# Decoder step on one core: last roundings of W_a on VectorE, first remainders of W_o on GpSimd, x in pairs, and a new order of norm and gate work

## The chip, the core and the metric

The kernel runs on one core of a Trainium2 chip. Five engines work side by side: PE (TensorE, matrix products), DVE (VectorE), ACT (ScalarE), POOL (GpSimd) and SP (SyncE, which here issues most of the loads and stores). Each takes its own instructions in the order written into the program, and waits where one needs something that another engine or a transfer has not delivered. The metric is device time in microseconds (us) of one launch; lower is better.

## The reference

One layer of a decoder for a prompt of 1024 tokens and 8 single-token samples, width 1024, all in 32-bit floats:

```
h  = RMSNorm(x) * (1 + scale1) + shift1
z  = h @ w_in                      # q,k,v, gates ga and gb, ...
y_a = W_a( gated delta rule )      # w_gdn_out
y_b = W_b( sliding-window attention )
x  = x + gate1 * W_o( sigmoid(ga) * y_a + sigmoid(gb) * y_b )
h2 = RMSNorm(x) * (1 + scale2) + shift2
x  = x + gate2 * W_down( silu(causal_dwconv3(h2 @ W_gate)) * (h2 @ W_up) )
final RMSNorm, and the new states
```

## The kernel before

Activations lie transposed: 128 partitions are 128 of the 1024 channels, a tile index j or k counts the 8 groups of channels, and the free axis holds the 1032 tokens (1024 of the prompt, 8 samples). W_a works in three parts of 384, 384 and 264 tokens (`PARTS`, t = 0, 1, 2), W_o in four quarters of 256, 256, 260 and 260 (`QUARTERS`, q). Two quarters are a half: `x1[0]` and `x1[1]` hold the residual of the two halves, 8 tiles each.

Every product is made in split form: an operand is taken apart into a rounding (hi, written as fp32r) and a remainder (lo = x − hi), and a product is three matmuls, hi·hi, hi·lo and lo·hi (`mm3`). The helper `split` issues the two steps: the rounding on ACT (L129), the remainder on DVE or on an engine that is passed to it (L130). In the profile a line of such a helper stands for many places, so the tile names tell the place: `wh`, `wl` are weights, `w` and `pk` weights or rooms of W_o and of the feed-forward part, `bmh` and `bml` the roundings and remainders of W_o's input, `mm` an accumulator in PSUM.

The stretch that the change touches has four pieces, one after the other:

1. The end of W_a (`ya_out` in `branches`). After each product of tile j and part t, DVE multiplies it by the gate (`sgx`), adds y_b's share into `t`, and `split` writes the rounding and remainder of the sum into `self.mix[q]`, one piece for each quarter that the part covers. That is `bmh` and `bml`: part 2 covers the last 4 columns of quarter 2 and all of quarter 3.
2. W_o (`output_pass`), quarter by quarter, 8 tiles in each. In quarter 0 each tile's weight is loaded too (`output_weights`, 512 KB into one of three `raw` buffers) and split: tile 0 into `w0` and `w1` in two halves of 512 columns, tile 2 into `w2` and `w3`, the others into rooms of `pk` that later hold other things. x's tile comes in by a load of its own (128 KB, L1431), is added to, and goes out to `x1d` (L1441). Tile 0's product in quarter 0 takes its three kinds of matmul in another order (L1439), the hi weights first.
3. The second norm (`second_norm`), for each quarter as a stream beside W_o: matmuls with ones sum the squares, DVE makes the mean (`rs`), POOL raises it to −1/2 (`power`, L125), DVE spreads it over a diagonal (`dg`, L1505), PE turns that into a row for all partitions (`nr`, L1506), and DVE and ACT scale x. `ffn_states` loads the convolution state (L1565) and transposes it on PE (`wv`, 128x88).
4. The gate and up projections (`ffn_gate_up`), which use seven products of sums and differences for a pair of weight tiles and a half of the tokens (`pair_product`). The seven operands of a half come from `operands`, those of the weights from `pair_weights`, whose sums (`ws`, L1589) are made on POOL for the gate weights.

These streams are written one after the other and given priorities (`weave`); a scheduler then merges them into one order for each engine, by its own cost estimates. So an instruction's place on an engine is not where it stands in the code. `issue_after` ties one instruction behind another on the scheduler's side.

Of the kernel before, what the change touches and what calls it, by code (L numbers as in the profile page):

```python
# [9 lines left out]
F32 = mybir.dt.float32  # L10
# [3 lines left out]
ALU = mybir.AluOpType  # L14
# [50 lines left out]
class Step:  # L65
# [56 lines left out]

    def power(self, out, in_, expo):
        e = expo[:in_.shape[0], :]
        self.nc.gpsimd.tensor_tensor(out, in_, e.broadcast_to(list(in_.shape)), op=ALU.pow)  # L125

    def split(self, hi, lo, x, eng=None):

        self.nc.scalar.activation(hi, x, AF.Copy)  # L129
        (eng or self.nc.vector).tensor_tensor(lo, x, hi.bitcast(F32), op=ALU.subtract)  # L130

    def load_split(self, pool, shape, src, tags, bufs, raws, home=None, raw=None):

# [1198 lines left out]
    def branches(self, pool, pool2):  # L1332
        nc, I = self.nc, self.I
        first = self.part_rooms(pool2, 0)
        ob = {**self.obX, 1: self.load_part(pool2, self.ob, 1)}
        ub = [self.t(pool, [P, KC, n], f"t{t}", bufs=1) for t, (_, n) in enumerate(PARTS)]
        samples, rows = self.sample_delta(pool2), self.last_rows()
        gate = lambda src, j, t: self.gate_part(pool if src is self.sga and j > 5 else self.gt[0], src[j][:, PARTS[t][0]:PARTS[t][0] + PARTS[t][1]], t)

        def yb_out(t, ps):  # L1340
            nc.vector.tensor_tensor(ub[t][:, j, :], ps, gate(self.sgb, j, t), op=ALU.mult)

        def ya_out(t, ps):
            u, v = ub[t][:, j, :], gate(self.sga, j, t)
            nc.vector.tensor_tensor(v, ps, v, op=ALU.mult)
            nc.vector.tensor_tensor(u, u, v, op=ALU.add)
            r0, n = PARTS[t]
            for q, (lo, m) in enumerate(QUARTERS):
                c, e = max(lo, r0), min(lo + m, r0 + n)
                if c < e:  # L1350
                    self.split(*(x[:, j, c - lo:e - lo] for x in self.mix[q]), u[:, c - r0:e - r0])
# [24 lines left out]
        self.bctx.close()  # L1376
        self.bm = self.pool("bm", 1, side="right")
        self.mix = [tuple(self.t(self.bm, [P, KC, QW], f"bm{x}{q}", F32R)[:, :, :n] for x in "hl")
                    for q, (_, n) in enumerate(QUARTERS)]
        for j0 in (0, 2, 4, 6):  # L1380
            w = [self.load_w(I["w_gdn_out"][0][:, j * P:(j + 1) * P]) for j in (j0, j0 + 1)]
            if 0 < j0 < 6:
                for j in (j0, j0 + 1):
                    self.project(w[j - j0], oa, ya_out)
                continue

            for ts in ((0,), (2,), (1,)) if j0 == 0 else ((0,), (1,), (2,)):
                for j in (j0, j0 + 1):
                    self.project(w[j - j0], oa, ya_out, ts)
# [17 lines left out]
    def output_pass(self, pool, q):  # L1407

        nc = self.nc
        lo, n = QUARTERS[q]  # L1410
        x1 = self.x1[q // 2][:, :, lo - HALF[q // 2][0]:][:, :, :n]

        def add(t, ps):
            self.add_gated(t, ps, j, 16)
            sq = self.t(pool, [P, QW], "nsq" if j else "nss", bufs=2)[:, :n]
            if q == 3 and j > 4:
                nc.vector.tensor_tensor(sq, x1[:, j, :], x1[:, j, :], op=ALU.mult)
            else:
                nc.scalar.activation(sq, x1[:, j, :], AF.Square)
            if j == 0:  # L1420
                self.squares[q] = [sq]
            elif j < 6:
                s = self.squares[q][0]
                nc.vector.tensor_tensor(s, s, sq, op=ALU.add)
            else:
                self.squares[q].append(sq)

        for j in range(8):
            if q == 0:
                self.wo.append(self.output_weights(j))  # L1430
            nc.sync.dma_start(x1[:, j, :], self.xT[j][:, lo:lo + n])  # L1431
            if q or j:
                self.project(self.wo[j], self.mix, add, parts=(q,), cols=QUARTERS)
            else:
                ps = self.t(self.next_mm(), [P, 512], "mm")[:, :n]
                (wh, wl), (xh, xl) = self.wo[0], self.mix[0]
                for i in range(3 * KC):
                    w, x, k = (wh, (xh, xl)[i % 2], i // 2) if i < 2 * KC else (wl, xh, i - 2 * KC)
                    nc.tensor.matmul(ps, w[:, k, :], x[:, k, :], start=i == 0, stop=i == 3 * KC - 1)  # L1439
                add(0, ps)  # L1440
            nc.sync.dma_start(self.x1d[j][:, lo:lo + n], x1[:, j, :])  # L1441
            yield

    def output_weights(self, j):

        src = self.I["w_o"][0][:, j * P:(j + 1) * P]
        raw = self.t(self.pw, [P, NP], "raw", bufs=3)
        self.nc.sync.dma_start(raw.rearrange("p (k c) -> p k c", k=KC), src.rearrange("(k p) c -> p k c", p=P))
        if j in (0, 2):
            w = [self.t(self.pw, [P, NP], tag, F32R, bufs=1) for tag in (f"w{j}", f"w{j + 1}")]  # L1450
        else:
            room = self.room(("pk0", "", "pk1", "pk2", "pk3", "pk4", "pk5")[j - 1], [P, KC * QW])
            w = room[:, :NP], room[:, NP:2 * NP]
        for c in (0, 512) if j == 0 else (slice(None),):
            c = c if j else slice(c, c + 512)
            self.split(*(x[:, c] for x in w), raw[:, c])
        return [x.rearrange("p (k c) -> p k c", k=KC) for x in w]

    def x1_cols(self, j, c, n):
# [19 lines left out]
    def second_norm(self, pool, psum, t):  # L1479
# [19 lines left out]
        for w, c0, c1 in ((P, 0, 2), (n - 2 * P, 2, nc_)):  # L1499
            if c0 < c1:  # L1500
                nc.vector.tensor_scalar(rs[:w, c0:c1], ss[:w, c0:c1], 1.0 / NP, EPS, op0=ALU.mult, op1=ALU.add)
        self.power(rs[:, :nc_], rs[:, :nc_], self.mhalf)
        yield
        dg = self.t(pool, [P, 3, P], "dg", bufs=1)[:, :nc_]
        nc.vector.tensor_tensor(dg, bc(self.ident, 1, nc_), bc(rs[:, :nc_], 2, P), op=ALU.mult)  # L1505
# [15 lines left out]
    def operands(self, pool, p, stage):  # L1521
# [18 lines left out]
        self.split(*ops[3], a1)  # L1540
        yield
        minus(d, b2, a1)
        self.split(*ops[2], d)
        yield
        minus(b1, b2, b1)
        self.split(*ops[4], b1)
        yield
        minus(a2, a2, d)
        self.split(*ops[5], a2)
        yield  # L1550
        self.split(*ops[6], b2)
        yield


# [19 lines left out]
        yield  # L1574
        nc.vector.tensor_tensor(sp, sp, bc(fcw[:, 3, :], 1, NS), op=ALU.add)

    def pair_weights(self, pool, w, f, eng=None):


        raw = []  # L1580
# [14 lines left out]
            self.split(t[:, 0], t[:, 1], x)  # L1595
            return t[:, 0], t[:, 1]

        out = [put(a0), put(b0)]
        s1 = calc(a1, b1, ALU.add)
        s2 = calc(s1, a0, ALU.subtract)  # L1600
        out += [put(s2), put(s1)]
        s3 = calc(a0, a1, ALU.subtract)
# [50 lines left out]
    def ffn_gate_up(self, pool, pool2, psum, f, w, first):  # L1653
# [9 lines left out]
        def gate(p, i, q, ps, r):  # L1663
            lo, n = QUARTERS[2 * p + q]
            zq = z[i][:, 2 + lo:2 + lo + n]
            if r is None:
                nc.scalar.copy(zq, ps)
            else:
                nc.vector.tensor_tensor(zq, ps, r, op=ALU.add)
            done[p, i] = done.get((p, i), 0) + 1  # L1670
            if done[p, i] == 2:
                conv(p, i)
# [19 lines left out]
            ss, r = self.norm_at  # L1692
            self.pair_product(psum, w, (0,), gate, {2: ss, 4: r})
        self.pair_product(psum, w, (1,) if first else (0, 1), gate)
        w = self.pair_weights(pool, I["w_ffn_up"][0], f, nc.vector if first else None)

        def up(p, i, q, ps, r):
            lo, n = QUARTERS[2 * p + q]
# [210 lines left out]
    def second_half(self):  # L1909

        nc, S = self.nc, ExitStack
        with S() as c:
# [6 lines left out]
            with S() as right:  # L1919
                xr = self.pool("xr", 1, ctx=right, side="right")  # L1920
                with S() as left:
                    xl = self.pool("xl", 1, ctx=left)
                    self.x1 = [self.t(pl, [P, KC, n], "x1") for pl, (_, n) in zip((xl, xr), HALF)]
                    self.x1d = self.t(self.dr, [KC, P, NT], "x1d")
                    self.squares, self.X, self.wo = {}, {}, []
# [151 lines left out]
```

## Time and profile before

| | us |
|---|---|
| median of 3 runs | 2076.88 (2074.53 to 2081.3) |
| the profiled execution | 2076.01 |
| its span | 2074.3 |
| PE busy | 2008.0 (97%) |
| PE waits for `dg` at L1506 | 3.0, once |
| PE waits for ACT's `w` at L1439 | 2.1, once |

The span runs from the first to the last instruction; 1.7 us of the execution lie around it. A row of the timeline has start, duration, engine, line, operation, out<-in and shape; a bracket behind it gives how long the engine was idle before it and what released it.

### The profile page before, as it was taken

What the parts mean: (1) busy time and instruction counts of PE and PEld (TensorE: products, weight loads), DVE (VectorE), ACT (ScalarE), POOL (GpSimd) and SP (SyncE); (2) the same over time, 40 slices, a digit from 0 to 9 for tenths busy, and PEclk for the clock granted to TensorE, in tenths of its full rate; (3) what the DMA queues carried; (4) which work ended last, traced back from release to release, by engine and by line L of the source; (5) the groups of instructions that cost most, each with busy time, mean ns of one, the idle gap of its engine ahead of it and who ended that gap; (6) DMA issues with size and microseconds to landing.
All of it is one profiled execution on the core that took longest, in us unless ns stands there. A gap on an engine that the chain in (4) does not pass through costs nothing.

```text
span 2074.3 us, 41298 instructions
## 1 busy us (share of the span) xinstructions
PE 2008.0 (97%) x16245; PEld 1905.2 (92%) x16245; DVE 1356.4 (65%) x2714; ACT 902.5 (44%) x2233; POOL 522.1 (25%) x594
## 2 busy tenths in 40 slices
PE   7999999999999999989989999999999999999998
PEld 4987877799999999979989999999999999999997
DVE  4755767483655746656554575479886777668866
ACT  4664545443334343442442452345544444444443
POOL 2000000131321211211111000004556556543561
PEclk9999999999999999999999999999999999999999
DMA  8256443332322322312276774513333332388783
GB/s 293 72 145 207 138 168 116 96 99 65 82 82 57 77 69 52 91 37 61 67 198 184 253 231 133 146 58 90 105 98 103 107 95 91 126 280 280 265 285 115
DMA packets 301887, 275.75 MB, mean 133 GB/s; under 512 B 59730, under 2 KB 248111, under 8 KB 301676
## 3 DMA queue, kind: packets, MB, share of 16 engines
q1 hardware_dynamic: 295642, 252.14, 39.7%
q0 software_dynamic: 5552, 20.37, 2.8%
q8 instruction: 127, 2.08, 0.4%
q14 instruction: 68, 0.56, 0.1%
q10 hardware_dynamic: 498, 0.61, 0.1%
HBM read 212.93 MB, written 62.51 MB: 133 GB/s over the span
## 4 chain that ended last, share of the span: by engine, by line
PE 82%; DMA 6%; DVE 6%; ACT 3%; issue 1%; SPq 1%; POOL 0%; DVEq 0%; POOLq 0%; ACTq 0%
PE mm L180 18%; PE mm L181 18%; PE mm L182 18%; PE wv L180 3%; PE wv L182 3%; PE wv L181 3%; PE wy L182 2%; PE wy L180 2%; PE wy L181 2%; PE pv L652 1%; DMA raw<-in_w_swa_out_dram 1%; PE pt L190 1%; PE tp L190 1%; PE mm L264 1%; PE sc L614 1%
## 5 line engine op out<-in xcount | busy, mean ns | idle before, releaser
L180 PE MATMUL mm<-b1h,wh 128*128 128x384 f32 (+1 forms) x1520 | 496.9, 328 | 4.0 <-ACT gt L1294 1.6
L181 PE MATMUL mm<-b1l,wh 128*128 128x384 f32 (+1 forms) x1520 | 489.1, 323 | 0.0
L182 PE MATMUL mm<-b1h,wl 128*128 128x384 f32 (+1 forms) x1520 | 487.7, 323 | 0.4 <-DVE wl L130 0.3
L180 PEld LDWEIGHTS mm<-b1h,wh 128*128 128x128 f32 x1520 | 286.5, 189 | 13.1 <-issue 4.6
L181 PEld LDWEIGHTS mm<-b1l,wh 128*128 128x128 f32 x1520 | 286.8, 189 | 4.4 <-issue 4.0
L182 PEld LDWEIGHTS mm<-b1h,wl 128*128 128x128 f32 x1520 | 286.0, 188 | 4.5 <-issue 2.8
L129 ACT ACTIVATE wh<-raw 128x1024 fp32r<-128x1024 f32 x83 | 87.1, 1050 | 124.4 <-PE mm L181 72.0
L130 DVE TENSOR_TENSOR wl<-raw,wh 128x1024 fp32r<-128x1024 f32 x82 | 101.9, 1244 | 59.8 <-ACT wh L129 58.9
L181 PE MATMUL mm<-pk,w 128*128 128x260 f32 (+1 forms) x440 | 124.3, 283 | 1.1 <-DVE pk L130 1.1
L180 PE MATMUL mm<-pk,w 128*128 128x260 f32 (+1 forms) x440 | 124.3, 283 | 0.0
L182 PE MATMUL mm<-pk,w 128*128 128x260 f32 (+1 forms) x440 | 124.1, 282 | 0.0
L130 DVE TENSOR_TENSOR w<-ws,w 128x512 fp32r<-128x512 f32 x88 | 78.2, 890 | 36.0 <-ACT w L129 35.8
L1626 ACT COPY bml<-mm 128x256 f32<-128x256 f32 (+1 forms) x132 | 48.9, 371 | 97.6 <-PE mm L182 94.5
L180 PE MATMUL mm<-bmh,w 128*128 128x260 f32 (+1 forms) x320 | 90.3, 282 | 0.0
L182 PE MATMUL mm<-bmh,w 128*128 128x260 f32 (+1 forms) x320 | 90.1, 282 | 0.0
L1681 DVE SCALAR_TENSOR_TENSOR fa<-fz,fcw,fa 128x512 f32<-128x512 f32 x88 | 74.5, 867 | 18.1 <-ACT fa L1679 17.8
L180 PE MATMUL mm<-b2h,wh 128*128 128x384 f32 (+1 forms) x256 | 83.2, 328 | 3.0 <-ACT wh L129 2.9
L181 PEld LDWEIGHTS mm<-pk,w 128*128 128x128 f32 x440 | 82.8, 188 | 1.3 <-DVE pk L130 1.3
L181 PE MATMUL mm<-b2l,wh 128*128 128x384 f32 (+1 forms) x256 | 83.6, 327 | 0.4 <-DVE b2l L130 0.4
L180 PEld LDWEIGHTS mm<-pk,w 128*128 128x128 f32 x440 | 82.9, 188 | 0.2 <-ACT bml L1626 0.2
L182 PEld LDWEIGHTS mm<-pk,w 128*128 128x128 f32 x440 | 82.9, 189 | 0.0
L182 PE MATMUL mm<-b2h,wl 128*128 128x384 f32 (+1 forms) x256 | 82.9, 326 | 0.0
(645 smaller groups left out, 5889.9 us busy)
## 6 DMA issues: line engine op xcount, KB each, us to landing
raw<-in_w_in_dram SPq DMA_DIRECT2D x59, 512.0 KB
ws<-in_w_ffn_down_dram SPq DMA_DIRECT2D x55, 256.0 KB
raw<-xd SPq DMA_DIRECT2D x47, 258.0 KB
raw<-in_w_ffn_down_dram SPq DMA_DIRECT2D x47, 256.0 KB
raw<-in_w_ffn_gate_dram SPq DMA_DIRECT2D x22, 512.0 KB
raw<-in_w_ffn_up_dram SPq DMA_DIRECT2D x22, 512.0 KB
qst<-in_w_mod_dram SPq DMA_DIRECT2D x16, 512.0 KB
raw<-in_w_mod_dram SPq DMA_DIRECT2D x16, 512.0 KB
```

The lines of the kernel that those rows point to most:

```text
L129: self.nc.scalar.activation(hi, x, AF.Copy)
L130: (eng or self.nc.vector).tensor_tensor(lo, x, hi.bitcast(F32), op=ALU.subtract)
L180: mm(ps, whi, xhi, start=first, stop=False, **kw)
L181: mm(ps, whi, xlo, start=False, stop=False, **kw)
L182: self.last_mm = mm(ps, wlo, xhi, start=False, stop=last, **kw).ins
L190: self.nc.tensor.transpose(out, in_, self.ident[:p, :p])
L264: nc.tensor.matmul(ps[32 * j:32 * j + 32], self.cT[:, k0 + j, :], ws[j // 2][:, j % 2, :], start=k0 == 0, stop=k0 > 0)
L614: self.scored = nc.tensor.matmul(sc[:, r, 256 - w:256], q, KH[:, lo:lo + w], start=True, stop=False)
L652: nc.tensor.matmul(pv[64 * r:64 * r + 64], V[:, n - back, ch], ps[:, r::2, :], start=back == 0, stop=back == (n > 0))
L1626: self.last_copy = nc.scalar.copy(r[p, i], x[p])
L1681: nc.vector.scalar_tensor_tensor(ai[:, c:e], zi[:, j + c:j + e], col(j), ai[:, c:e], op0=ALU.mult, op1=ALU.add)
```

## The change

Five edits go together.

- In W_a's last part (t = 2) the tiles j = 6 and 7 no longer round on ACT: DVE writes the rounding itself, as a second sum with an fp32r output, and then the remainder. Other tiles are as before.
- The remainders of W_o's tiles 0 and 1 go to POOL instead of DVE.
- x is loaded two tiles at a time (256 KB and 260 KB), at even j.
- In the gate weights' first use, a weight sum is tied behind the second quarter's `power`.
- The seven gate operands of the second half are tied together in the order in which the products take them: the third operand first, the fifth and sixth behind it, the seventh last. Two copies out of PSUM in the first gate product move from ACT to DVE, one addition waits for the last square of the norm, and one operand of the first up weight waits for the third operand.

```diff
     def split(self, hi, lo, x, eng=None):
-        self.nc.scalar.activation(hi, x, AF.Copy)
-        (eng or self.nc.vector).tensor_tensor(lo, x, hi.bitcast(F32), op=ALU.subtract)
+        return (self.nc.scalar.activation(hi, x, AF.Copy),
+                (eng or self.nc.vector).tensor_tensor(lo, x, hi.bitcast(F32), op=ALU.subtract))
+    def behind(self, made):
+        stack = ExitStack()
+        for x in made:
+            stack.enter_context(self.tc.issue_after(x.ins))
+        return stack
...
         def ya_out(t, ps):
             u, v = ub[t][:, j, :], gate(self.sga, j, t)
             nc.vector.tensor_tensor(v, ps, v, op=ALU.mult)
...
+            if t < 2 or j < 6:
+                nc.vector.tensor_tensor(u, u, v, op=ALU.add)
+                for rooms, a, b, m in spans:
+                    self.split(*(x[:, j, a:a + m] for x in rooms), u[:, b:b + m])
+                return
+            for (hi, _), a, b, m in spans:
+                nc.vector.tensor_tensor(hi[:, j, a:a + m], u[:, b:b + m], v[:, b:b + m], op=ALU.add)
             nc.vector.tensor_tensor(u, u, v, op=ALU.add)
+            for (hi, lo), a, b, m in spans:
+                nc.vector.tensor_tensor(lo[:, j, a:a + m], u[:, b:b + m], hi[:, j, a:a + m].bitcast(F32), op=ALU.subtract)
...
-            nc.sync.dma_start(x1[:, j, :], self.xT[j][:, lo:lo + n])
+            if j % 2 == 0:
+                nc.sync.dma_start(x1[:, j:j + 2, :], self.xT[j:j + 2, :, lo:lo + n].rearrange("k p n -> p k n"))
...
-            self.split(*(x[:, c] for x in w), raw[:, c])
+            self.split(*(x[:, c] for x in w), raw[:, c], None if j > 1 else self.nc.gpsimd)
...
-        self.power(rs[:, :nc_], rs[:, :nc_], self.mhalf)
+        self.factors.append(self.power(rs[:, :nc_], rs[:, :nc_], self.mhalf))
...
-        self.split(*ops[2], d)
+        made = self.split(*ops[2], d)
         yield
-        minus(b1, b2, b1)
-        self.split(*ops[4], b1)
+        self.third = made if p else ()
+        with self.behind(self.third):
+            minus(b1, b2, b1)
+            self.split(*ops[4], b1)
         yield
-        minus(a2, a2, d)
-        self.split(*ops[5], a2)
+        with self.behind(self.third):
+            minus(a2, a2, d)
+            made = self.split(*ops[5], a2)
         yield
-        self.split(*ops[6], b2)
+        with self.behind(made if p else ()):
+            self.split(*ops[6], b2)
...
-        out = [put(a0), put(b0)]
-        s1 = calc(a1, b1, ALU.add)
+        out = [put(a0)]
+        with self.behind(after):
+            out.append(put(b0))
+        with self.behind(self.factors[1:2] if f == 0 and len(self.factors) == 3 else ()):
+            s1 = calc(a1, b1, ALU.add)
...
-                nc.scalar.copy(zq, ps)
+                (nc.vector.tensor_copy if first and not p else nc.scalar.copy)(zq, ps)
             else:
-                nc.vector.tensor_tensor(zq, ps, r, op=ALU.add)
+                with self.behind([self.last_square] if first and not p else ()):
+                    nc.vector.tensor_tensor(zq, ps, r, op=ALU.add)
...
-        w = self.pair_weights(pool, I["w_ffn_up"][0], f, nc.vector if first else None)
+        w = self.pair_weights(pool, I["w_ffn_up"][0], f, *((nc.vector, self.third) if first else ()))
```

What the scheduler makes of it shows in the order of each engine. A row has the line, the operation, out<-in and the shape; numbers behind a name tell buffers apart.

ACT at the turn from W_a to W_o, before (`bmh2` and `bmh3` are the roundings of W_a's sums for quarters 2 and 3, `t2` the sums of part 2, `w0`, `pk0` and `w2` the roundings of W_o's tiles 0, 1 and 2):

```order
L129 ACTIVATE bmh2_2117_13460<-t1_2039_12683 128x256
L129 ACTIVATE bmh2_2117_13460<-t2_2040_12684 128x4
L129 ACTIVATE bmh3_2119_13462<-t2_2040_12684 128x260
L129 ACTIVATE bmh2_2117_13460<-t2_2040_12684 128x4
L129 ACTIVATE bmh3_2119_13462<-t2_2040_12684 128x260
L129 ACTIVATE w0_2200_14338<-raw_2199_14336 128x512 x2
L129 ACTIVATE pk0_2205_14376<-raw_2204_14374 128x1024
L129 ACTIVATE w2_2209_14412<-raw_2208_14410 128x1024
```

And now:

```order
L129 ACTIVATE bmh2_2117_13460<-t1_2039_12683 128x256
L129 ACTIVATE w0_2200_14338<-raw_2199_14336 128x512 x2
L129 ACTIVATE pk0_2205_14376<-raw_2204_14374 128x1024
L129 ACTIVATE w2_2209_14411<-raw_2208_14409 128x1024
L1434 ACTIVATE nss_2203_14371<-x1_2196_14333 128x256
```

The four roundings of part 2 are gone from ACT, and W_o's first rounding follows directly on the last rounding of part 1.

SP's loads at the same place, before (`raw<-in_w_o_dram` are W_o's tiles 0, 1, 2, 3 and so on; `x1<-xT` loads x, `x1d<-x1` stores it):

```order
L1448 DMA raw_2208_14410<-in_w_o_dram 128x8x128
L1431 DMA x1_2196_14333<-xT_154_950 128x256 x6
L1448 DMA raw_2213_14447<-in_w_o_dram 128x8x128
L1431 DMA x1_2196_14333<-xT_154_950 128x256 x3
L1448 DMA raw_2217_14483<-in_w_o_dram 128x8x128
L1431 DMA x1_2196_14333<-xT_154_950 128x256 x2
L1448 DMA raw_2221_14519<-in_w_o_dram 128x8x128
L1441 DMA x1d_2198_14335<-x1_2196_14333 128x256
L1431 DMA x1_2196_14333<-xT_154_950 128x256 x5
```

And now:

```order
L1464 DMA raw_2208_14409<-in_w_o_dram 128x8x128
L1447 DMA x1_2196_14333<-xT_154_950 128x2x256 x8
L1464 DMA raw_2213_14446<-in_w_o_dram 128x8x128
L1447 DMA x1_2197_14334<-xT_154_950 128x2x260 x4
L1464 DMA raw_2217_14481<-in_w_o_dram 128x8x128
L1457 DMA x1d_2198_14335<-x1_2196_14333 128x256
L1464 DMA raw_2221_14517<-in_w_o_dram 128x8x128
L1447 DMA x1_2197_14334<-xT_154_950 128x2x260 x4
L1457 DMA x1d_2198_14335<-x1_2196_14333 128x256 x2
```

Between tiles 2 and 3 of W_o stood six single tiles of x; now eight pairs stand there, the whole first half, and the second half's pairs follow in two groups of four.

POOL from the last gate load (`sgx`) on, before (`ws` are the gate weights' sums, `rs` the norm's power):

```order
L1393 DMA sgx_2192_14296<-sga_445_2614 128x264
L1589 TENSOR_TENSOR ws_2319_15523<-raw_2315_15513,raw_2316_15515 128x512
L1589 TENSOR_TENSOR ws_2320_15525<-ws_2319_15523,raw_2315_15513 128x512
L1589 TENSOR_TENSOR ws_2323_15533<-raw_2315_15513 128x512
L125 TENSOR_TENSOR rs_2291_15396<-rs_2291_15396,mhalf_90 128x2
L125 TENSOR_TENSOR rs_2301_15431<-rs_2301_15431,mhalf_90 128x2
```

And now:

```order
L1408 DMA sgx_2192_14296<-sga_445_2614 128x264
L130 TENSOR_TENSOR w1_2201_14339<-raw_2199_14336,w0_2200_14338 128x512 x2
L130 TENSOR_TENSOR pk0_2205_14376<-raw_2204_14374,pk0_2205_14376 128x1024
L125 TENSOR_TENSOR rs_2291_15380<-rs_2291_15380,mhalf_90 128x2
L125 TENSOR_TENSOR rs_2301_15415<-rs_2301_15415,mhalf_90 128x2
L1609 TENSOR_TENSOR ws_2319_15507<-raw_2315_15497,raw_2316_15499 128x512
```

The remainders of tiles 0 and 1 came in, and both powers moved ahead of the weight sums. On PE, W_o's tile 2 now comes ahead of most of tile 1, the state's transposes stand in front of the rest of tile 6, behind quarter 1's tile 0, and quarter 0's `nr` product comes 10 matmuls earlier in quarter 1.

More of the change, by code (lines that the diff above doesn't have):

```diff
@@ L124, in power @@
         e = expo[:in_.shape[0], :]
-        self.nc.gpsimd.tensor_tensor(out, in_, e.broadcast_to(list(in_.shape)), op=ALU.pow)
+        return self.nc.gpsimd.tensor_tensor(out, in_, e.broadcast_to(list(in_.shape)), op=ALU.pow)
     def split(self, hi, lo, x, eng=None):
-        self.nc.scalar.activation(hi, x, AF.Copy)
-        (eng or self.nc.vector).tensor_tensor(lo, x, hi.bitcast(F32), op=ALU.subtract)
+        return (self.nc.scalar.activation(hi, x, AF.Copy),
[5 more added lines that the diff above has]
+        return stack
     def load_split(self, pool, shape, src, tags, bufs, raws, home=None, raw=None):
@@ L1345, in ya_out @@
             nc.vector.tensor_tensor(v, ps, v, op=ALU.mult)
[L1346 to L1351, printed above, removed]
+            r0, n = PARTS[t]
+            spans = [(self.mix[q], max(lo, r0) - lo, max(lo, r0) - r0, min(lo + m, r0 + n) - max(lo, r0))
+                     for q, (lo, m) in enumerate(QUARTERS) if max(lo, r0) < min(lo + m, r0 + n)]
+            if t < 2 or j < 6:
[5 more added lines that the diff above has]
+                nc.vector.tensor_tensor(hi[:, j, a:a + m], u[:, b:b + m], v[:, b:b + m], op=ALU.add)
+            nc.vector.tensor_tensor(u, u, v, op=ALU.add)
+            for (hi, lo), a, b, m in spans:
+                nc.vector.tensor_tensor(lo[:, j, a:a + m], u[:, b:b + m], hi[:, j, a:a + m].bitcast(F32), op=ALU.subtract)
         weights = lambda j: self.load_w(I["w_swa_out"][0][:, j * P:(j + 1) * P])
@@ L1416, in add @@
             if q == 3 and j > 4:
-                nc.vector.tensor_tensor(sq, x1[:, j, :], x1[:, j, :], op=ALU.mult)
+                self.last_square = nc.vector.tensor_tensor(sq, x1[:, j, :], x1[:, j, :], op=ALU.mult)
             else:
@@ L1575, in ffn_states, with pair_weights @@
         nc.vector.tensor_tensor(sp, sp, bc(fcw[:, 3, :], 1, NS), op=ALU.add)
-    def pair_weights(self, pool, w, f, eng=None):
+    def pair_weights(self, pool, w, f, eng=None, after=()):
         raw = []
@@ L1924, in second_half @@
                     self.x1d = self.t(self.dr, [KC, P, NT], "x1d")
-                    self.squares, self.X, self.wo = {}, {}, []
+                    self.squares, self.X, self.wo, self.factors = {}, {}, [], []
                     norm = lambda q: self.second_norm(xr, psum, q)
```

## The prediction

> **What bounds the kernel now.** I read the page's busy times first, then a table of windows over the stretch that the change touches (1280 to 1440 us), then the timeline of each engine there.
>
> ```profile
> PE 2008.0 (97%) x16245; PEld 1905.2 (92%) x16245; DVE 1356.4 (65%) x2714; ACT 902.5 (44%) x2233; POOL 522.1 (25%) x594
> 1285.00:1290.00 5.00, 4.98 (x29) 4.98 (x30) 4.00 (x7) 2.39 (x3) 0.00 (x0) 0.66 0.88 253
> 1290.00:1300.00 10.00, 10.00 (x88) 10.00 (x87) 5.70 (x9) 4.36 (x7) 0.00 (x0) 1.00 1.07 317
> 1320.00:1330.00 10.00, 6.95 (x57) 6.69 (x56) 4.47 (x8) 3.22 (x7) 3.95 (x4) 1.00 0.09 28
> 1400.00:1410.00 10.00, 9.02 (x70) 8.37 (x69) 9.66 (x14) 9.97 (x17) 0.00 (x0) 1.00 0.19 53
> 1410.00:1420.00 10.00, 8.40 (x67) 8.09 (x68) 10.00 (x14) 3.83 (x8) 2.35 (x2) 1.00 0.33 106
> 1430.00:1440.00 10.00, 9.28 (x77) 9.07 (x76) 9.97 (x14) 3.76 (x8) 8.73 (x10) 1.00 0.26 80
> ```
>
> The columns after the window are its length, the busy time of PE, PEld, DVE, ACT and POOL, then PE's granted clock, the DMA share and GB/s. PE is busy 97% of the span, so only PE's holes count, and no multiplication is removed. The holes in reach are few. In 1285 to 1290 the clock is 0.66. In 1320 to 1330 PE lacks 3.05 us. In the last three rows it lacks 0.98, 1.60 and 0.72 us, 3.3 together, while DVE has no time left. From 1290 to 1300 PE is full, but so is the DMA: its share is 1.07 at 317 GB/s.
>
> The first hole is the turn from W_a to W_o:
>
> ```profile
> 1278.39 0.62 ACT L129 ACTIVATE bmh<-t 128x128 fp32r<-128x128 f32 x2 [3.54 <-DVE t L1346]
> 1282.68 0.28 PE L182 MATMUL mm<-b2h,wl 128*128 128x264 f32 x1
> 1283.47 0.43 DVE L1346 TENSOR_TENSOR t<-t,sgx 128x264 f32<-128x264 f32 x1
> 1283.94 0.52 ACT L129 ACTIVATE bmh<-t 128x4 fp32r<-128x4 f32 x2 [2.38 <-DVE t L1346]
> 1284.36 1.14 ACT L129 ACTIVATE w<-raw 128x512 fp32r<-128x512 f32 x2
> 1285.02 0.49 PE L1439 MATMUL mm<-bmh,w 128*128 128x256 f32 x1 [2.06 <-ACT w L129]
> 1285.53 0.41 PE L1439 MATMUL mm<-bmh,w 128*128 128x256 f32 x1
> 1285.74 0.41 PE L1439 MATMUL mm<-bml,w 128*128 128x256 f32 x1
> 1288.52 1.13 PE L1439 MATMUL mm<-bmh,w 128*128 128x256 f32 x8
> ```
>
> ACT runs in order. W_o's first rounding (w) stands behind the roundings (bmh) of W_a's last tile, which wait for DVE's sum, which waits for PE's last W_a product. So PE waits for itself. At full clock, 0.12 us a matmul (the last row: 1.13 less the 0.28 that one lasts, over 7), W_o would start at 1282.80; it starts at 1285.02, 2.2 us late. Then the matmuls come 0.21 apart until 1288.52: 17 of them in 3.50 us where 2.04 would do, 1.5 us more. The turn costs 3.7 us.
>
> The second hole is quarter 0's norm:
>
> ```profile
> 1315.64 0.16 DVE L1501 TENSOR_SCALAR rs<-nr 128x2 f32<-128x2 f32 x1 [2.42 <-PE nr L1496]
> 1319.50 1.28 POOL L1589 TENSOR_TENSOR ws<-raw,raw 128x512 f32<-128x512 f32 x1 [40.31 <-DMA raw<-in_w_ffn_gate_dram]
> ...
> 1322.08 1.26 POOL L1589 TENSOR_TENSOR ws<-raw 128x512 f32<-128x512 f32 x1
> 1323.30 0.73 POOL L125 TENSOR_TENSOR rs<-rs,mhalf 128x2 f32<-128x2 f32 x1
> 1324.54 0.70 PE L1506 MATMUL nr<-dg,ones 128*128 128x256 f32 x2 [3.05 <-DVE dg L1505]
> ```
>
> DVE's mean (L1501) is there at 1315.8, but the power (rs on POOL) stands behind three weight sums (the middle one left out here), which waited for the gate weights' DMA until 1319.50. PE loses 3.05 us, from 1321.5. The clock stays 1.00 here.
>
> **The change, part by part.** *The last roundings of W_a (tiles 6 and 7) on VectorE.* Four ACT instructions (0.52 us for each pair) become four DVE sums of the same shapes, at most 0.43 each like the 264-column sum, about 1.5 us in all. They stand behind PE's W_a products; what they feed, quarters 2 and 3, is multiplied after quarters 0 and 1 (16 tiles of 24 matmuls at 0.12, 46 us). Cost on the path 0. ACT is free from about 1279.0 (the first row) and rounds w and the first pk before W_a ends, so W_o starts at 1282.80: −3.7 us at this place.
>
> *W_o's first remainders on GpSimd.* POOL has no timed two-input 128x1024 subtraction. From below it costs DVE's price, 1.23 (row further down), from above three of the 128x512 sums at 1.28, 3.8; I take two, 2.6, the nearest row doubled. With the two 128x512 ones POOL works 5.2 us, from about 1279.6 to 1284.8. PE wants the first two after 16 matmuls, 1284.7, and has them at about 1282.2. It wants the third after some 49 matmuls, 1288.7. The cover is 2.5 us and 3.9 us; if it went, each microsecond of lateness would be swallowed by the later wait for W_o's fourth tile, worked out next.
>
> A rule speaks against this part. The Trainium skill, page "GPSIMD Engine Reference", section 4.1, gives elementwise work to VectorE, since two-input operations are about twice as slow on GpSimd. The trace agrees (1.28 us here against DVE's 1.23 for twice the columns). By that rule this would be 2.5 us lost; by the slack in the rows it is 0, and the sum keeps the rows.
>
> *x two tiles a load.* This is the part with a price. In the new order SP issues eight pair loads, all of x's first half (2.1 MB), ahead of W_o's fourth tile (j=3); before, six 128 KB loads stood there. Then come four pairs of the second half ahead of j=4, and four more ahead of j=6.
>
> ```profile
> 1283.00 2.71 SPq L1431 DMA_DIRECT2D x<-xT  x6
> 1286.35 0.39 SPq L1448 DMA_DIRECT2D raw<-in_w_o_dram  x1
> 1286.80 1.51 SPq L1431 DMA_DIRECT2D x<-xT  x3
> 1288.42 0.38 SPq L1448 DMA_DIRECT2D raw<-in_w_o_dram  x1
> 1288.85 1.82 SPq L1431 DMA_DIRECT2D x<-xT  x2
> 1290.76 0.38 SPq L1448 DMA_DIRECT2D raw<-in_w_o_dram  x1
> 1291.47 1.39 SPq L1441 DMA_DIRECT2D x1d<-x  x1
> 1292.91 2.38 SPq L1431 DMA_DIRECT2D x<-xT  x5
> 1295.38 0.38 SPq L1448 DMA_DIRECT2D raw<-in_w_o_dram  x1
> 1291.49 1.06 ACT L129 ACTIVATE pk<-raw 128x1024 fp32r<-128x1024 f32 x1 [0.81 <-DMA raw<-in_w_o_dram]
> 1300.55 1.06 ACT L129 ACTIVATE pk<-raw 128x1024 fp32r<-128x1024 f32 x1 [0.27 <-DMA raw<-in_w_o_dram]
> 1292.59 1.23 DVE L130 TENSOR_TENSOR pk<-raw,pk 128x1024 fp32r<-128x1024 f32 x1 [2.42 <-ACT pk L129]
> sgx<-sga POOLq DMA_DIRECT2D x2, 132.0 KB, 2.4
> sgx<-sga POOLq DMA_DIRECT2D x1, 192.0 KB, 4.5
> ```
>
> The two ACT rows start when tiles 3 and 6 of W_o land. Between them, in 9.06 us, came what SP issued between their loads: ten x loads, one x1d store and three W_o loads, 3.0 MB, or 333 GB/s. I take them to land in the order of issue. The last two rows (the list of DMA issues, 1268 to 1312 us) end with the time from issue to landing. At 333 GB/s a pair costs 0.79 us (0.80 with 260 columns), a W_o tile 1.58, an x1d store 0.39. The first bytes come 2.0 us after the issue (2.4 for 132 KB, less its own 0.4), so at 1285.0; x is still bound to the last W_a product by its buffers, 1283.00.
>
> - j=3 lands at 1285.0 + 8 × 0.79 + 1.58 = 1292.9 (before: 1291.49). Its remainder is ready 2.33 later (1291.49 to 1292.59 + 1.23), at 1295.2. PE has done three tiles by 1282.8 + 72 × 0.12 = 1291.4 and wants that remainder at its third matmul, 1291.7: a wait of 3.5 us.
> - j=4 lands after four pairs more, 1292.9 + 3.2 + 1.58 = 1297.7; remainder 1300.0. PE wants it at 1298.1: 1.9 us.
> - j=5, behind one store: 1299.6, remainder 1301.9; PE wants it at 1302.9. No wait.
> - j=6, behind four pairs and two stores: 1305.2; its rounding is ready at 1306.3, PE wants it at 1305.5: 0.8 us.
> - The state load behind j=7 (1307.2) feeds transposes that now stand in front of the rest of tile 6, wanted at 1309.4. The load lands 0.5 (176 KB at 333 GB/s) to 4.5 us (the 192 KB load's row) later, at 1309.7 in the middle: 0.3 us, with ends 0 and 2.3.
>
> Together +6.5 us. Between 1283 and 1306 the DMA, not PE, then sets the pace: 6.72 MB stand ahead of tile 6's landing. The ends follow from the rate: at 253 GB/s, the row of 1285 to 1290, they take 26.6 us instead of 20.2, +6.4; at 341 GB/s or so, −0.5. The half clock may follow a wait again; a 1.5 us loss after the first wait would only shorten the second (1.9).
>
> The Trainium skill, page "TensorE: Matmul & The Clock Gate", section "Why this matters for your kernels", wants no PE gaps over about 3 us, as one idle window brings half clock back. The trace differs both ways: 2.06 us idle was followed by half clock, 3.05 us was not. By the page the turn would have cost 2.2 us and the norm 4.6; the sum goes by the rows.
>
> *Weight sums behind the powers.* Then nothing stands ahead of the power but the remainders, long done. By the rows' own times it would end 0.73 after 1315.8, the product with it (dg) on DVE some 0.5 later, at 1317.1; PE asks at 1321.5, or at 1320.3 since the new order asks 10 matmuls earlier. −3.1 us. The sums wait for quarter 1's power, some 23 us later (8 tiles); what they feed is multiplied only after quarters 2 and 3, another 46 us, so 0.
>
> *Gate operands in order of use.*
>
> ```profile
> 1410.51 0.39 PE L180 MATMUL wv<-bml,w 128*128 128x256 f32 x1 [1.11 <-ACT w L129]
> 1412.10 0.39 PE L181 MATMUL mm<-pk,w 128*128 128x260 f32 x1 [1.09 <-DVE pk L130]
> 1407.56 1.24 DVE L1538 TENSOR_TENSOR x<-x,td 128x1040 f32<-128x1040 f32 x1
> 1409.05 1.24 DVE L130 TENSOR_TENSOR bmh<-x,bmh 128x1040 fp32r<-128x1040 f32 x1
> 1410.80 1.25 DVE L130 TENSOR_TENSOR pk<-td,pk 128x1040 fp32r<-128x1040 f32 x1
> ```
>
> The third operand's remainder (last row) now comes ahead of the two DVE rows above it, so both waits can go, 2.2 us of the 3.3. But DVE is full, and two copies out of PSUM (ACT's before) move onto it, about 0.9 us; the fifth to seventh operands come later instead. Ends: −3.3 and +0.9; near the middle −1.2.
>
> **Sum** on the profiled execution (2076.01 us, 2074.3 of span): −3.7 − 3.1 − 1.2 + 6.5 = −1.5, so 2074.5 us. It lay 0.9 us under the median of the three runs, 2076.88; 0.3% of that, 6.2 us, is about what a measurement can tell from no change: faster is under 2070.7, slower over 2083.1.
>
> **The rivals.** *Full gain:* the x loads hide, W_o's tiles come in time: 2076.0 − 3.7 − 3.1 − 1.2 = 2068.0 (2065.9 if all 3.3 go). For it: ACT's wait for tile 3 cost PE nothing before. Against: it needs 6.72 MB in 13.9 us, 480 GB/s; no row shows over 341. *Slower:* the pairs come at a lower rate, because of their two-row layout. 253 GB/s gives 2080.9; from 233 GB/s, 8.6 us more than I forecast, it is over 2083.1. For it: the row with 253; against: SP's 0.45 us an issue bounded that row, and a pair needs one issue for two tiles. *The gate stage gives nothing:* DVE, at 9.66 to 10.0 of 10, is slowed by the copies: −3.7 − 3.1 + 0.9 + 6.5 = +0.6, 2076.6.
>
> **How the numbers follow.** Forecast 0.62, gate stage without gain 0.18, full gain 0.13, slower 0.07. Faster 0.18 (the full gain and the forecast's lower tail), slower 0.07, same 0.75. Range: 2070.0 (forecast with all of the gate stage and 341 GB/s or a little more) to 2079.5 (about 265 GB/s); outside lie the full gain and the slow pairs.
>
> **What would show it.** Right: W_o's first matmul follows W_a's last at once; PE then waits for DVE's remainder of tile 3 near 1291.5 and tile 4 near 1298, ACT's pk rows released by DMA; no wait ahead of nr near 1322; the roundings of w on ACT near 1279. Wrong: tile 3's rounding before 1291; a wait for POOL's w in the first 50 matmuls; a longer wait in front of the transposes; DVE's gate operands late for other tiles.

## The result

The changed kernel is slower by a little: 2082.88 us (median of 22 runs) against 2078.44 (22 runs of before), ratio 1.0023 with a 95% interval of 1.0013 to 1.0032, which is 2.7 to 6.7 us. I had forecast 1.5 us less and a range up to 2079.5. Of the 3.4 us beyond that range 1.6 lie in before itself, whose first three runs had a median of 2076.88. The profiled execution of the changed kernel took 2088.76 us, a long one: W_a's last matmul begins at 1290.6 us in it, at 1282.2 and 1282.6 in two later profiles of the same kernel, so 8 us of its excess lie ahead of all changed code. I therefore compare stretches of the traces, not spans. The measure used from here on is the time on PE from the start of W_a's last matmul to the start of the 201st matmul that writes wy, an accumulator in PSUM of the gate and up products; there, in the third pair of gate and up weights, both kernels run the same order again. I call it the stretch. Its first part, up to the first matmul into wy, holds W_o and the norms; the rest is the gate stage. It is 267.4 us before and 269.1 us now: 1.8 us more where the forecast had 1.5 less.

The windows of the changed kernel (columns as before) show where PE lacks time. On the clock of this trace W_a ends 8 us later than before:

```profile
1285.00:1290.00 5.00, 5.00 (x44) 5.00 (x43) 3.75 (x8) 3.56 (x6) 3.01 (x3) 1.00 0.10 27
1290.00:1300.00 10.00, 7.68 (x54) 7.48 (x53) 6.69 (x13) 0.42 (x1) 2.92 (x2) 0.85 0.82 252
1300.00:1310.00 10.00, 7.49 (x55) 6.73 (x55) 4.57 (x8) 4.15 (x6) 0.00 (x0) 0.98 1.14 330
```

The first row still lies in W_a. In the 20 us that follow W_a's end PE lacks 2.3 and 2.5 us, and the clock drops to 0.85. The timeline of the turn, engine by engine:

```profile
1290.59 0.29 PE L189 MATMUL mm<-b2h,wl 128*128 128x264 f32 x1
1290.72 0.28 PE L1455 MATMUL mm<-bmh,w 128*128 128x256 f32 x1
1296.56 0.39 PE L189 MATMUL mm<-bmh,w 128*128 128x256 f32 x1 [2.32 <-DVE w L130]
1287.53 2.81 POOL L130 TENSOR_TENSOR w<-raw,w 128x512 fp32r<-128x512 f32 x2 [0.42 <-ACT w L129]
1290.29 2.62 POOL L130 TENSOR_TENSOR pk<-raw,pk 128x1024 fp32r<-128x1024 f32 x1
1288.01 0.43 DVE L1352 TENSOR_TENSOR sgx<-mm,sgx 128x264 f32<-128x264 f32 x1 [0.64 <-PE mm L189]
1289.22 1.41 DVE L1364 TENSOR_TENSOR t<-t,sgx 128x264 f32<-128x264 f32 x1
1290.66 2.62 DVE L1366 TENSOR_TENSOR bml<-t,bmh 128x4 fp32r<-128x4 f32 x2
1294.66 0.50 DVE L1366 TENSOR_TENSOR bml<-t,bmh 128x4 fp32r<-128x4 f32 x2
1295.28 1.23 DVE L130 TENSOR_TENSOR w<-raw,w 128x1024 fp32r<-128x1024 f32 x1
```

W_o starts 0.13 us after W_a's last matmul, as forecast. Then PE waits 2.32 us for DVE's remainder of tile 2, a wait that the forecast did not have, and half clock follows. DVE was not short of work to do; it stood still. The 264-column sum (L1364), 0.43 us before, takes 1.41 and ends 0.3 us after POOL's second half-tile. The pair of subtractions (L1366), 0.50 us a few rows below, takes 2.62: its first, 128x4, ends at 1292.94, within 0.02 us of POOL's 128x1024 subtraction, and only then does the second run. The product by the gate at 1288.01, one of whose inputs comes from PSUM, runs beside POOL at its usual 0.43.

The loads, and the first tile that waits for them:

```profile
1290.91 4.18 SPq L1447 DMA_DIRECT2D x<-xT  x8
1295.20 0.41 SPq L1464 DMA_DIRECT2D raw<-in_w_o_dram  x1
1302.39 1.06 ACT L129 ACTIVATE pk<-raw 128x1024 fp32r<-128x1024 f32 x1 [5.00 <-DMA raw<-in_w_o_dram]
1304.04 1.22 DVE L130 TENSOR_TENSOR pk<-raw,pk 128x1024 fp32r<-128x1024 f32 x1
1305.31 0.38 PE L189 MATMUL mm<-bmh,pk 128*128 128x256 f32 x1 [1.30 <-DVE pk L130]
```

Tile 3 lands 11.8 us after W_a's last matmul began (11.4 and 11.1 in the later profiles); the forecast had 10.2.

The norm of quarter 0:

```profile
1329.26 0.16 DVE L1517 TENSOR_SCALAR rs<-nr 128x2 f32<-128x2 f32 x1 [0.42 <-PE nr L1512]
1329.50 0.73 POOL L125 TENSOR_TENSOR rs<-rs,mhalf 128x2 f32<-128x2 f32 x1 [36.59 <-DVE rs L1517]
1332.92 0.59 PE L1522 MATMUL nr<-dg,ones 128*128 128x256 f32 x2
```

The power follows the mean within 0.1 us and PE does not wait (no bracket on its row).

All waits on PE from 1270 to 1460 us (us in total, times, longest):

```profile
PE mm L189 <- DVE pk L130: 2.5, 2, 1.3
PE mm L189 <- DVE w L130: 2.3, 1, 2.3
PE mm L187 <- DVE fa L1727: 1.6, 1, 1.6
PE mm L187 <- ACT pk L129: 1.3, 2, 1.0
PE mm L187 <- ACT bml L1649: 0.7, 2, 0.5
PE wv L187 <- ACT pk L129: 0.4, 1, 0.4
```

The first two rows and 0.3 of the fourth lie in W_o. The rest, 3.7 us, lies in the gate stage. The two waits there that the gate order was to remove (1.11 and 1.09) are gone, but others have come: 1.0 and 0.4 for ACT's roundings of gate operands (pk), 0.7 for bml, and 1.6 for DVE's multiplication by the up product (fa). Before, the stage had 3.2 us of waits.

### The profile page after: what moved, and what is told of

Same layout as the page of the kernel before. It is cut to its first block, busy times and chain, and to the rows that moved or that the text cites. A ratio compares the mean times of both kernels' runs of the same rounds, so it can differ in the third digit from the quotient of the medians.

```text
span 2087.1 us, 41285 instructions
## 1 busy us (share of the span) xinstructions
PE 2018.0 (97%) x16245; PEld 1915.8 (92%) x16245; DVE 1355.8 (65%) x2716; ACT 902.3 (43%) x2228; POOL 528.2 (25%) x597
## 4 chain that ended last, share of the span: by engine, by line
PE 77%; DVE 8%; DMA 7%; ACT 3%; issue 2%; SPq 2%; POOL 1%; DVEq 0%; POOLq 0%; ACTq 0%
PE mm L187 17%; PE mm L188 17%; PE mm L189 17%; PE wv L187 2%; PE wv L189 2%; PE wv L188 2%; PE pv L659 1%; PE wy L189 1%; PE wy L187 1%; PE wy L188 1%; PE pt L197 1%; PE tp L197 1%; PE mm L271 1%; DMA ws<-in_w_ffn_down_dram 1%; DVE x L1488 1%
```

## The experiments

Theory 1: the x pairs ahead of W_o's tiles 3, 4 and 6 hold these back on the way in. Theory 2: GpSimd's remainders hold up VectorE. They differ in which single part, undone, gives the time back. Then come tests of the order of the loads alone, of the gate order, and two more profiles of each kernel.

| kernel | stretch, us | of it up to the first wy | half-clock windows: up to the first wy + gate stage | time against before, 95% interval |
|---|---|---|---|---|
| before, three profiles | 267.4, 267.2, 265.6 | 104.6, 103.8, 102.6 | 1+0, 0+1, 0+1 | 1 |
| changed, three profiles | 269.1, 269.4, 269.8 | 106.5, 106.7, 106.4 | 1+0, 1+0, 1+1 | 1.0023 [1.0013, 1.0032] |
| e1 single x loads | 265.2 | 101.4 | 0+1 | 0.9998 [0.9984, 1.0012] |
| e2 remainders on VectorE | 268.5 | 104.7 | 0+1 | 1.0006 [0.9993, 1.0019] |
| e3 both | 264.4 | 100.6 | 0+0 | 0.9985 [0.9972, 0.9998] |
| e4 gate order undone | 272.7 | 109.0 | 2+0 | 1.0021 [1.0009, 1.0032] |
| e5 x late | 265.5 | 102.2 | 1+1 | 1.0004 [0.9989, 1.0019] |
| e6 x late, remainders on VectorE | 262.6 | 99.9 | 0+0 | 0.9982 [0.9968, 0.9995] |
| e9 as e6, gate order undone | 266.5 | 101.1 | 0+1 | 0.9999 [0.9989, 1.001] |
| e10 as e6, single x loads | 263.9 | 100.1 | 0+0 | 0.9983 [0.997, 0.9996] |

A half-clock window (granted clock 0.50) lasts 3.4 us in each of these traces and costs about 1.5, as at the turn before.

**e1, x tile by tile.**

```diff
-            if j % 2 == 0:
-                nc.sync.dma_start(x1[:, j:j + 2, :], self.xT[j:j + 2, :, lo:lo + n].rearrange("k p n -> p k n"))
+            nc.sync.dma_start(x1[:, j, :], self.xT[j][:, lo:lo + n])
```

> The changed kernel with x loaded tile by tile again (eight 128 KB loads ahead of W_o's fourth tile instead of eight of 256 KB); the rest of the change stays. Measure: time on PE from W_a's last matmul to the 201st matmul into wy, 267.4 us before and 269.1 us changed. Theory 1, the x pairs hold back W_o's tiles 3, 4 and 6 on the way in: about 1 MB less stands ahead of tile 3, so it lands 2.5 to 4 us earlier and the measure falls to about 265 to 266. Theory 2, GpSimd's remainders hold up VectorE: the wait of 2.3 us for tile 2's remainder and its half clock stay, the measure stays at 268.5 or more.

Measured: 265.2, as theory 1 said, 4.0 us less than the changed kernel. Two of its waits on PE (us in total, times, longest), those for W_o, and DVE's sum:

```profile
PE mm L189 <- DVE w L130: 2.3, 1, 2.3
PE mm L189 <- DVE pk L130: 0.3, 1, 0.3
1284.65 1.40 DVE L1364 TENSOR_TENSOR t<-t,sgx 128x264 f32<-128x264 f32 x1
```

Tile 2's wait (w) is there unchanged, with DVE's sum at 1.40; no half clock followed it this time. What went are the waits for pk, W_o's later tiles. The order has eight x loads ahead of tile 3 in both kernels; as pairs they carry twice the bytes.

**e2, remainders of tiles 0 and 1 on VectorE.**

```diff
-            self.split(*(x[:, c] for x in w), raw[:, c], None if j > 1 else self.nc.gpsimd)
+            self.split(*(x[:, c] for x in w), raw[:, c])
```

> The changed kernel with the remainders of W_o's tiles 0 and 1 back on VectorE; pairs and the rest stay (the order then has six pairs ahead of tile 3 instead of eight). Theory 1 (pairs hold back W_o): PE's wait for tile 2 goes, but PE stands longer at tile 3; of 269.1 us only what the two pairs less bring, about 1.5, goes: 267 to 268. Theory 2 (GpSimd holds up VectorE): the 264-column sum on VectorE falls from 1.41 to about 0.43 us, the wait at tile 2 with its half clock goes, 269.1 falls by 3 or more, to 265 to 266.

Measured: 268.5 in the stretch, 0.7 us less, nearer to theory 1's 267 to 268 than to theory 2's 265 to 266. VectorE's rows are as theory 2 said:

```profile
1286.10 0.43 DVE L1364 TENSOR_TENSOR t<-t,sgx 128x264 f32<-128x264 f32 x1
1286.56 0.50 DVE L1366 TENSOR_TENSOR bml<-t,bmh 128x4 fp32r<-128x4 f32 x2
1287.93 1.34 PE L1455 MATMUL mm<-bmh,w 128*128 128x256 f32 x8 [0.96 <-DVE w L130]
1297.57 0.39 PE L189 MATMUL mm<-bmh,pk 128*128 128x256 f32 x1 [0.76 <-DVE pk L130]
PE mm L187 <- ACT pk L129: 2.0, 2, 1.0
PE mm L189 <- DVE pk L130: 2.0, 4, 0.8
```

Freed of POOL, the same instructions take 0.43 and 0.50 again. PE's wait at tile 2 becomes one of 0.96 at tile 0, and 2.9 us of waits for later tiles take up part of what was won (the other 1.0 us for ACT's pk lies in the gate stage). PE gets past tile 3's remainder 12.8 us after W_a, where the forecast had 12.6 and the changed kernel 14.7. Up to the first wy e2 is 1.8 us shorter than the changed kernel (104.7 against 106.5), with no half clock there; the 0.7 of the whole stretch counts in a half-clock window of the gate stage that the changed kernel's first profile doesn't have. So both mechanisms are there, one behind the other.

**e3, both edits of e1 and e2 at once.**

> The changed kernel with x tile by tile and the remainders on VectorE: of the change there stay the last roundings on VectorE, the weight sums behind the power, and the gate operands. Both theories: the turn (3.7 us) and the norm (3.1 us) are won, and W_o's tiles come in the order of before, so PE meets tile 3 about 2 to 3 us too early; the measure is 262 to 264.5, the time 3 to 5 us under before. If it is not under 266, something else in the change costs the time.

Measured: 264.4, inside the expected 262 to 264.5, and the time is 0.15% under before (interval 0.02 to 0.28%). What is left of the change is worth having.

**e4, the gate operands as before** (`behind` and the two copies of `ffn_gate_up` undone, the rest of the change kept).

```diff
-        with self.behind(self.third):
-            minus(b1, b2, b1)
-            self.split(*ops[4], b1)
+        minus(b1, b2, b1)
+        self.split(*ops[4], b1)
...
-                (nc.vector.tensor_copy if first and not p else nc.scalar.copy)(zq, ps)
+                nc.scalar.copy(zq, ps)
```

> The changed kernel with the gate operands, the two copies and the tied instructions as before; pairs, GpSimd's remainders, roundings and the power's place stay. If the gate order saves nothing, as the waits of the changed kernel (4.6 us in that stage against 4.3) say, the measure stays within 0.5 us of 269.1 and the time within 0.05% of the changed kernel's. If the order costs: 268 or less. If it saves what I forecast (1.2 us): 270.3.

Measured: 272.7, over all three expectations; two half-clock windows fell into it, both in W_o (at 1291 and 1373), which the edit does not touch. In the gate stage, free of half clock in both, it takes 163.7 us against 162.7 in the changed kernel. That is no measure of the gate order by itself: e3 and e10, which have it, take 163.8 there without half clock too, and before, which doesn't, 162.7. The whole time, 1.0021, cannot be told from the changed kernel's.

**e5, x late.** The changed kernel, with x of quarters 1 to 3 tied behind W_o's last load.

```diff
+        self.wo_load = self.nc.sync.dma_start(raw..., src...)
...
-                nc.sync.dma_start(x1[:, j:j + 2, :], ...)
+                with self.tc.issue_after(self.wo_load.ins) if q else nullcontext():
+                    nc.sync.dma_start(x1[:, j:j + 2, :], ...)
```

> The changed kernel with one thing more: the x loads of quarters 1 to 3 are tied behind the load of W_o's last tile, so that only the four pairs of quarter 0 stand ahead of W_o's tile 3. GpSimd's remainders and all else stay. Measure as before: from W_a's last matmul to the 201st into wy (267.4 before, 269.1 changed, 265.2 with single loads). Theory 1 (the x pairs ahead of W_o's tiles cost the time): about 1 MB less ahead of tile 3 and 4 MB less ahead of tile 6; no wait for tiles 3 to 6 by DMA is left, but GpSimd still holds up VectorE, so the 2.3 us wait at tile 2 stays: 263 to 265. Theory 2 (GpSimd alone): no change, 268.5 or more.

Measured: 265.5 with two half-clock windows, 0.5 over theory 1's range and 3.6 us under the changed kernel's first profile, which has one. The list of waits on PE up to 1400 us is short:

```profile
PE mm L189 <- DVE w L130: 2.3, 1, 2.3
PE mm L187 <- ACT bml L1650: 0.5, 1, 0.5
```

No wait for pk is left: with four pairs ahead instead of eight, W_o's tiles come in time. The edit touches the loads' order alone (the scheduler moves a few other instructions with it, such as quarter 0's nr, 27 matmuls earlier on PE), so theory 1 is shown. The wait of theory 2 stays, 2.3 us, and the half clock after it.

**e6, x late, and the remainders on VectorE** (the edits of e2 and e5).

> As e5, and the remainders of W_o's tiles 0 and 1 back on VectorE. Both causes are then gone while the pairs stay as pairs: if they are the whole cause, no wait of over 0.5 us for W_o is left but the 1.0 us at tile 0 that single loads with VectorE showed; the measure is 260 to 262.5 and the time 0.2 to 0.35% under before. If pairs as such are slow, or if something else costs, it stays over 264.

Measured: 262.6, just over the expected range, no half-clock window, and the time is 0.18% under before (0.05 to 0.32%), just short of the 0.2 expected. Its two longest waits up to 1400 us, and the loads:

```profile
PE mm L1456 <- DVE w L130: 1.0, 1, 1.0
PE mm L187 <- ACT bml L1650: 0.5, 1, 0.5
1285.98 1.90 SPq L1448 DMA_DIRECT2D x<-xT  x4
1289.40 2.64 SPq L1465 DMA_DIRECT2D raw<-in_w_o_dram  x3
1293.57 1.06 ACT L129 ACTIVATE pk<-raw 128x1024 fp32r<-128x1024 f32 x1 [1.03 <-DMA raw<-in_w_o_dram]
```

Tile 3 lands 7.9 us after W_a instead of 11.8. Of the versions tried this one has the shortest stretch. Its time is under that of before and of the changed kernel; e3 and e10 lie within its interval.

**e9, e6 with the gate order of before** (the edits of e4 on top).

> As e6 (x of quarters 1 to 3 behind W_o, remainders on VectorE), with the gate operands, copies and tied instructions as before. From the first matmul into wy to the 201st: 162.7 us in the kernel before, in the changed one and in e6. If the gate order saves nothing, 162.7 again; if it saves the 1.0 us by which e4 (gate order undone) was over the changed kernel, 163.7, and the time about 0.05% over e6.

Measured: 165.4 from the first wy to the 201st, with one half-clock window that e6 does not have; less 1.5 it is 163.9 against 162.7. With pairs, then, the stage is 1.0 and 1.2 us longer without the gate order (e4, e9); with single loads it is 163.8 with the order (e3, e10) and 162.7 without (before). The whole times do not agree either: undoing the order costs nothing in e4 (2082.5 us against 2082.9) and 4.4 us in e9 (2078.7 against 2074.2). So it isn't shown that the gate order saves time as such.

**e10, e6 with single x loads.**

> As e6, with single x loads instead of pairs, those of quarters 1 to 3 still behind W_o's last tile. If only the bytes ahead of W_o's tiles matter, pairs or singles make no difference: from W_a's last matmul to the first into wy 99.9 us as in e6, within 1. If a pair is better or worse as such (SP's issue of 0.45 us each), it differs by more.

Measured: 100.1 us from W_a's last matmul to the first wy, against 99.9 in e6. In this part pairs or singles make no difference once those of quarters 1 to 3 do not stand ahead of W_o; what counts is the bytes. The whole stretch is 1.3 us longer than e6's, nearly all of it in the gate stage (163.8 against 162.7).

**e7 and e12, the kernel before again; e8 and e11, the changed kernel again.** No edit.

> The kernel before, profiled a second time, to see how far the measure repeats: if it is a property of the order it lies within 0.3 us of 267.4, apart from 1.6 us for each half-clock window that falls into it or out of it; the wait in W_down near 750 us after W_a, 1.5 us in the first profile, may differ.

> The kernel before a third time: the measure 267.2 again within 0.3, apart from half-clock windows; the W_down wait 1.7 to 1.9 if it belongs to the order, more if it is chance.

> The changed kernel, profiled a second time: 269.1 again within 0.3 us if the waits are set by the order; tile 2's wait of about 2.3 us and VectorE's sums stretched to about 1.4 us return. If the W_down wait (2.8 us in the first profile) belongs to the change it returns at 2.5 or more; if it is chance it may be near the 1.5 of before.

> The changed kernel a third time, for the wait in W_down some 750 us after W_a (loss on PE 3.0 and 1.7 in two profiles; with GpSimd's remainders in three other kernels 4.9, 3.5, 3.3; without them 1.7, 1.9, 1.9, 2.9, 1.7). If it belongs to GpSimd's remainders: 3 or more. If it is chance: anywhere from 1.7 to 4.9. The measure to the 201st wy: 269.2 again.

Measured: the changed kernel repeats (269.4, 269.8). The kernel before repeats in length once (267.2) and misses once (265.6), and even in the 267.2 its parts differ. In the second and third profile the window 1285 to 1290 has no half clock, and the norm's wait is shorter. A window and two rows of the waits of the second profile, then two of the third:

```profile
1285.00:1290.00 5.00, 4.73 (x39) 4.74 (x40) 4.25 (x8) 3.06 (x5) 0.00 (x0) 1.00 0.83 245
PE nr L1506 <- DVE dg L1505: 1.7, 1, 1.7
PE mm L182 <- DVE pk L130: 0.8, 1, 0.8
```

```profile
PE nr L1506 <- DVE dg L1505: 1.4, 1, 1.4
PE mm L182 <- DVE pk L130: 0.8, 1, 0.8
```

Without half clock at the turn PE meets tile 6 of W_o early and waits 0.8 there for its remainder; the norm's wait is 1.7 and 1.4 where the first profile had 3.05. The wait in W_down cost PE 1.7, 1.9 and 3.1 us in the three profiles of before and 3.0, 1.7 and 2.6 in those of the changed kernel. The spread within each kernel is as large as between them, so this wait is not the change's.

## Why the prediction was wrong

Three terms of the sum failed: the gains at the turn and the norm were added up from one profile and too large, the gate order's gain did not show, and the remainders on GpSimd, put at 0, cost time. The main term, the pairs ahead of W_o's tiles, was there by the mechanism that I gave, but smaller than my 6.5 us; that the cost in W_o came out near 6.5 all the same is luck.

- *The turn:* right at its place; W_o follows W_a at once (2.2 us). The 1.5 us of half clock behind it came in one of the three profiles of before.
- *The norm:* right, PE no longer waits. The 3.05 us were the longest of three. Together the two removed holes cost 6.8 us in the profile that I read, but 5.1 (2.2 + 0.4 + 0.8 + 1.7) and 4.4 (2.2 + 0.8 + 1.4) in the others, the waits at tile 6 included. They aren't independent either: the waits at tile 6 are there only where no half clock followed the turn. The mean is 5.4; my terms had 6.8.
- *W_o's loads:* forecast 6.5 us of new waits for tiles 3, 4 and 6. The waits for pk are 2.8, 3.1 and 3.0 us in the three profiles of the changed kernel; tile 3 took 1.3, 1.9 and 1.5 of them instead of 3.5, since PE came there late, held at tile 2. Moving or halving the loads gave back 3.6 to 4.8 us up to the first wy (changed to e1, less one half clock; changed to e5; e2 to e3 and to e6). With tile 2's wait and its half clock (2.3 + 1.5), W_o's new cost is 6.6, 6.9 and 6.8 us, 0.3 over my term in the mean: the part that I missed filled the part that I had too large.
- *GpSimd's remainders cost 0:* this step failed. I took POOL's durations well (2.81 for the two, 2.62 for the third) but asked only for POOL's own lateness; I did not ask what POOL's work does to VectorE. VectorE stood still for 3 us (1.41 and 2.62 where 0.43 and 0.50 are usual), and tile 2's remainder came late. Back on VectorE they save 0.8 to 2.3 us up to the first wy (e1 to e3, changed to e2, e5 to e6), though a wait of 1.0 at tile 0 comes in; in the last two pairs 1.5 of it is half clock. The whole times go the same way in all three pairs, by 2.3 to 4.3 us, with intervals that overlap. Half clock followed directly in four of the six profiles with these remainders on GpSimd (in a fifth behind tile 3's wait); W_o had none in the five with them on VectorE. "Swallowed by the later wait" held only in part: PE got past tile 3 after 13.8 to 14.7 us, not 12.6.
- *Gate operands, −1.2:* this failed too. From the first wy to the 201st the stage takes 162.7 us in the first profiles of before and of the changed kernel alike, and 163.0 and 162.9 in the means of three. The waits for w and the third operand went, as forecast, but those for pk and fa that came in their place are as long (3.7 us against 3.2 in all). I had named this as the rival "the gate stage gives nothing" and as a sign of being wrong, with a chance of 0.18.
- *One-column matmuls:* the nine that sum quarter 2's squares now stand one by one between the products' matmuls; before, seven of them stood in a row. I left that out. From quarter 1's nr to quarter 2's the changed kernel takes 1.8 us more, of which its later place (10 matmuls at 0.12) is 1.2. Every kernel here with pairs has this order, and none with single loads: it comes with the pairs.

Put together: −1.5, plus 1.4 for the holes, 1.2 for the gate stage, 0.3 for W_o and 0.6 for the one-column matmuls is +2.0 us. The mean of three stretches rose by 2.7, from 266.7 to 269.4. e6, where both costs in W_o are gone, checks the gains: up to the first wy it is 3.8 us under the mean of before, which is 5.4 for the holes less 1.0 for the wait at tile 0 and 0.6 for the one-column matmuls; my rival "full gain" had 6.8 there. The time rose by 4.4, with an interval from 2.7; whether the rest is more than spread is open.

The rival "slower" had the right side and the wrong reason. The 252 GB/s from 1290 to 1300 count some 2 us before the first bytes; from 2 to 10 us after W_a's last matmul the DMA moved 327 to 329 GB/s in the three profiles, near the 333 that I counted with. By 10.2 us, when I had tile 3 landing, 2.8 MB had come, and up to tile 3 the order has 2.6 MB. It landed 0.9 to 1.6 us later even so; my assumption that loads land in the order of issue may have failed there, but no run tests that.

## What to carry to other kernels

When an instruction is moved to an idle engine, price it at both ends: its own duration there, and what the neighbours' instructions take while it runs. When transfers are merged, look at the order by bytes, not by count: what is needed first must be ahead; one tie on the loads' order (e5) won 3.6 us of the stretch. Take a second profile of the kernel before adding up its holes, and a sum that comes out right may hide two errors: undo the parts one by one.

## What the hardware showed that I had not expected

In these traces POOL's two-input subtraction holds VectorE's instructions with both inputs in SBUF until it ends: a 128x4 subtraction that takes 0.16 us alone took 2.28 and ended with POOL's. One with an input in PSUM was not held (0.43 us beside POOL). The Trainium skill, page "GPSIMD Engine Reference", section 1 (Specifications), says that GpSimd's SBUF interfaces are shared with VectorE, with contention for instructions with two SBUF inputs; the trace agrees, and shows the size. The profile of before had it already, in the gate stage:

```profile
1420.61 1.67 POOL L1589 TENSOR_TENSOR ws<-ws,raw 128x512 f32<-128x512 f32 x1 [0.68 <-DVE w L130]
1421.05 1.26 DVE L1685 SCALAR_TENSOR_TENSOR fa<-fz,fcw,fsp 128x8 f32<-128x8 f32 x1
1424.71 0.22 DVE L1685 SCALAR_TENSOR_TENSOR fa<-fz,fcw,fsp 128x8 f32<-128x8 f32 x1
```

The same 128x8 instruction takes 1.26 us beside POOL's sum and 0.22 alone. I had read POOL's rows for their durations and not DVE's beside them.

Half clock after a hole is not a matter of the hole's length alone: the same 2.06 us at the turn brought it in one of three profiles. In e4 the window at 1373 came without a hole: PE was busy for all of 1370.0 to 1373.4, where the nine one-column matmuls stand.
